# Three kinds of stores of a hybrid decoder kernel are issued from ACT's queue instead of SP's

## The chip, the cores and the metric

The kernel runs on one core of one Trainium2 chip. The time is the device time of one execution in microseconds; a kernel is judged by the median of its runs. Before the change three runs took 1882.16, 1882.66 and 1893.46 us, so the median is 1882.66 us. One execution was profiled.

The core has five engines that run their own instruction streams: PE (matmuls, with PEld for its weight loads), ACT (activations, copies and casts, one input element after the other on 128 partitions), DVE (vector arithmetic), POOL and SP. Each engine has a sequencer, which reads the engine's instructions in order, waits for semaphores and hands the work on. In this kernel SP computes nothing: its sequencer only issues DMA transfers. POOL's issues DMA transfers too, above all the row gathers. ACT's issues none before the change.

## The reference

One layer of a hybrid decoder is applied to 512 prompt tokens and 64 sampled tokens (8 sequences of 8), 576 rows of 1024 floats, all in fp32:

```
proj  = rmsnorm(x) @ w_in                    # q, k, v for 12 heads of 64, and the three conv parts
attn  = merge of three dilated sliding-window attentions (the sample tokens read a cache of 2048 keys)
conv  = B * causal_conv3(C * H)
h     = x + [rmsnorm(attn) | rmsnorm(conv)] @ w_out
xn    = rmsnorm(h)
s     = product keys of xn @ wq              # 8 heads, two halves of 128 keys each
eid,g = top 16 of the 16 x 16 sums per head, softmax over the 16
out   = h + sum over the 128 (head, expert) pairs of g * gelu(xn . u[eid]) * v[eid]
y     = rmsnorm(out)
```

There are 16384 experts, each with one row of u and one of v, of 1024 floats. The outputs are y for both token sets, the new k and v rows, and the conv states.

## The kernel before, in words

The 576 rows are five blocks (`BLKS`): four prompt blocks of 128 rows and the sample block of 64. Precision comes from splitting each fp32 operand into a rounded high part and a rest (`split`, L102 to L104: ACT makes the high part, DVE the rest) and from three matmuls for each product.

The layer's tail (the experts, "PEER") is done in two ways. Blocks 0 and 4 gather, for every one of the 128 pairs, the u and v rows by indirect DMAs from POOL, with dot products and sums on DVE (`gather_units`, L469 to L487). Blocks 1 to 3 (`DENSE`, 384 tokens) use all experts: a matrix G of the gate values, mostly zero, is multiplied into gelu(U x), and the result into V.

The dense way has 128 chunks of 128 experts:

- `ustep(i)` (L773) loads a 512 KB chunk of u to tile `ur` (two buffers, L767, SP), splits it to `uh` and `ul` (two buffers each), does 24 matmuls into `pu` (L107 to L109), and takes the gelu on ACT to tile `a` (L782, 128 x 384). For chunks 0 to 67 (`LAG`) the result must wait until G is ready. Chunks 62 to 67 keep it in SBUF, and chunks 0 to 61 store it to DRAM as `Ad[i]`, 192 KB each, from one of three buffers (L786). These are the stores of U results.
- `gbuild` (L812) makes G for one dense block at a time. For 8 tokens at a time DVE makes one-hot matrices (L844, L848), ACT multiplies the rest of the gate values into them (`oi`, L852, eight activations of 128 x 128), PE multiplies them (`pG`, L857 and L858), and ACT moves the results to `stg` (L860, two activations of 128 x 512). After 32 tokens `stg` (two buffers of 2 MB) is stored as `Gd[...]` (L863). There are 12 of these stores of gates. The loop at L866 calls `ustep` between the pieces of `gbuild`.
- From L933 on, the V stage: U steps 68 to 127 and V steps alternate. Each V step loads a chunk of v, reads back its part of `Gd` (L891) and, for the first 62 chunks, `Ad` (L896), multiplies them on DVE, splits, and does 18 matmuls (L909 to L913).

Ahead of this, `group` (L576) does the output projection, residual and second norm, for block 0 alone and then for blocks 1 to 4. Its inner function `second` (L616) stores the residual rows of a block as `hd` (L619, up to 512 KB, five stores), and goes on with the norm, whose first instruction is a square on ACT (`norm_block`, L157). `hd` is read only at the end (`finish`, L923).

The order of the instructions in each engine's queue is not the order of the text. A planner puts them in order when the program is built, from modelled times: an instruction takes its place when its inputs are modelled as ready, and among ready ones the earlier in the text goes first. On the chip each queue is then strictly in order. A DMA instruction stands in the queue of the engine that issues it, and its wait for the tile that it stores stands there with it. The waits themselves are put in by the builder. Each DMA signals one of eight semaphores for SP's and ACT's transfers together, used in turn, so the issue of one also waits until the earlier user of its semaphore has landed.

Of the kernel before, what the change touches and what calls it, by code (L numbers as in the profile page):

```python
# [19 lines left out]
P = 128  # L20
# [19 lines left out]
TB = 32  # L40
# [27 lines left out]
def body(tc, I, O):  # L68
    nc = tc.nc
# [14 lines left out]
    hd = dram.tile([NTOK, D], F32, name="hd")  # L84
    Ad = dram.tile([LAG, P, ND], F32, name="Ad")
    Gd = dram.tile([NTB, P, NCH, TB], F32, name="Gd")
# [19 lines left out]
    def mm3(out, ah, al, bh, bl, first, last):  # L106
        nc.tensor.matmul(out, ah, bh, start=first, stop=False)  # L107
        nc.tensor.matmul(out, ah, bl, start=False, stop=False)  # L108
        nc.tensor.matmul(out, al, bh, start=False, stop=last)  # L109
# [44 lines left out]
    def norm_block(src, n, gb, out):  # L154
        ss = small.tile([P, 1], F32, name="ss")
        jk = small.tile([P, D], mybir.dt.bfloat16, name="jk", bufs=1)
        nc.scalar.activation(jk[:n], src, AF.Square, accum_out=ss[:n])  # L157
        r = small.tile([P, 1], F32, name="rr")
        rsqrt(r[:n], ss[:n], 1.0 / D, n, 1)
        nc.vector.scalar_tensor_tensor(out, src, r[:n], gb[:n], op0=OP.mult, op1=OP.mult)  # L160

    def transpose_split(xn, n, hi, lo, ps):
        for hf in range(2):
            pt = ps.tile([P, 4, P], F32, name="pT")
            for k in range(4):
                c = hf * 4 + k
                nc.tensor.transpose(pt[:, k, :n], xn[:n, c * P:(c + 1) * P], ident[:n, :n])
            split(hi[:, hf * 4:hf * 4 + 4, :], lo[:, hf * 4:hf * 4 + 4, :], pt[:, :, :n])
# [279 lines left out]
    def pump(cost):  # L448
        credit[0] += cost
        while bg and credit[0] > 0:  # L450
            try:
                c = next(bg[0])
                credit[0] -= c
                left[0] -= c
            except StopIteration:
                bg.pop(0)
        if not bg:
            credit[0] = 0.0
# [117 lines left out]
    def group(grp, st, chp, clp, mm, psc, x2dst, lname, pre2=None):  # L576
# [10 lines left out]
        h = gp.tile([P, nb, D], F32, name="h")  # L587
        for bi, b in enumerate(grp):
            t0, n = BLKS[b]
# [7 lines left out]
        for part, (c0, c1) in enumerate(((0, 6), (6, 8))):  # L597
# [4 lines left out]
            for bi, b in enumerate(grp):  # L602
                t0, n = BLKS[b]
# [12 lines left out]
        def second(bi):  # L616
            b = grp[bi]
            t0, n = BLKS[b]
            nc.sync.dma_start(hd[t0:t0 + n, :], h[:n, bi, :])  # L619
            x2 = x2dst.get(b) if b in x2dst else gp.tile([P, D], F32, name="x2t", bufs=2)  # L620
            norm_block(h[:n, bi, :], n, g2b, x2[:n])
            sl = slice(t0 - g0, t0 - g0 + n)
            transpose_split(x2, n, chp[:, :, sl], clp[:, :, sl], psU)
            pump(PUMP_GB * 2)

        for co in range(2):
            for part, dps in ((1, (3,)), (0, (0, 1, 2))):
# [12 lines left out]
                for bi, b in enumerate(grp):  # L640
                    t0, n = BLKS[b]
# [11 lines left out]
        if one:  # L653
            second(0)
# [8 lines left out]
        if len(grp) == 1:  # L663
            b = grp[0]
            t0, n = BLKS[b]
# [24 lines left out]
        for cc in range(16):  # L690
# [10 lines left out]
            for bi, b in enumerate(grp):  # L701
                t0, n = BLKS[b]
# [5 lines left out]
            for bi, b in enumerate(grp):  # L708
                n = BLKS[b][1]
# [55 lines left out]
    def load_split(src, pl, tag):  # L765
        raw = pl.tile([P, D], F32, name=tag + "r", bufs=RB[tag])
        nc.sync.dma_start(raw, src)  # L767
        hi = pl.tile([P, D], F32R, name=tag + "h")
        lo = pl.tile([P, D], F32R, name=tag + "l")
        split(hi, lo, raw)  # L770
        return hi, lo

    def ustep(i):  # L773
        uh, ul = load_split(I["ut"][i], up, "u")
        uh = uh.rearrange("p (c e) -> p c e", e=P)
        ul = ul.rearrange("p (c e) -> p c e", e=P)
        ps = pu[0].tile([P, 512], F32, name="pu", bufs=2)
        for dc in range(DC):
            mm3(ps[:, :ND], uh[:, dc, :], ul[:, dc, :], x2h[:, dc, :ND], x2l[:, dc, :ND], dc == 0, dc == DC - 1)
        kept = LAG - KEEP <= i < LAG  # L780
        a = up.tile([P, ND], F32, name=f"a{i}" if kept else "a", bufs=1 if kept else AB)
        nc.scalar.activation(a, ps[:, :ND], AF.Gelu)  # L782
        if kept:
            akeep[i] = a
        elif i < LAG:
            nc.sync.dma_start(Ad[i], a)  # L786
        return a

    def unext():
        if ui[0] < LAG:  # L790
            ustep(ui[0])
            ui[0] += 1
            pump(PUMP_WIN)
# [18 lines left out]
    def gbuild(di, b):  # L812
        ef = tk.tile([P, SLOTS], F32, name="ef", bufs=2)
        gt = tk.tile([P, SLOTS], F32, name="gt", bufs=2)
        yield from topk2(st, b, P, ef, gt)
        ei = tk.tile([P, SLOTS], I32, name="ei")
        ii = tk.tile([P, SLOTS], I32, name="ii")
        ij = tk.tile([P, 2, SLOTS], F32, name="ij")
        nc.vector.tensor_copy(ei, ef)
        nc.vector.tensor_scalar(ii, ei, 7, None, op0=OP.logical_shift_right)  # L820
        nc.vector.tensor_copy(ij[:, 0, :], ii)
        nc.vector.tensor_scalar(ii, ei, 127, None, op0=OP.bitwise_and)
        nc.vector.tensor_copy(ij[:, 1, :], ii)
        pt = psG.tile([P, 4, P], F32, name="pT")
        nc.tensor.transpose(pt[:, 0, :], ij[:, 0, :], ident)
        nc.tensor.transpose(pt[:, 1, :], ij[:, 1, :], ident)
        nc.tensor.transpose(pt[:, 2, :], gt, ident)
        JT = gbp.tile([P, P], F16, name="JT")
        J4 = gbp.tile([P, 2, P, 4], F16, name="J4")
        gs = gbp.tile([P, P], F32, name="gs", bufs=1)  # L830
        gl = gbp.tile([P, P], F32, name="gl")
        nc.vector.tensor_copy(JT, pt[:, 1, :])
        nc.vector.tensor_copy(J4[:, 0], pt[:, 0, :].unsqueeze(2).to_broadcast([P, P, 4]))
        nc.vector.tensor_scalar(gs, pt[:, 2, :], GSC, None, op0=OP.mult)
        nc.vector.tensor_copy(J4[:, 1], gs.unsqueeze(2).to_broadcast([P, P, 4]))
        nc.vector.tensor_tensor(gl, gs, J4[:, 1, :, 0], op=OP.subtract)
        yield 1.5
        for tb in range(P // TB):
            stg = gbp.tile([P, NCH, TB], F32, name="stg")
            for q in range(TB // TQ):  # L840
                c0 = tb * TB + q * TQ
                cs = slice(c0, c0 + TQ)
                oj = gbp.tile([P, P, TQ], F16, name="oj")
                nc.vector.tensor_tensor(oj, iotaj, JT[:, cs].unsqueeze(1).to_broadcast([P, P, TQ]), op=OP.is_equal)  # L844
                OI = [gbp.tile([P, 32, TQ, 4], F16, name=f"oi{k}") for k in range(3)]
                f = "p a t b -> p a (t b)"
                for k, in0, op in ((0, iotax, OP.is_equal), (1, OI[0], OP.mult)):
                    nc.vector.tensor_tensor(OI[k].rearrange(f), in0.rearrange(f),  # L848
                                            J4[:, k, cs, :].rearrange("p t b -> p (t b)").unsqueeze(1)
                                            .to_broadcast([P, 32, TQ * 4]), op=op)  # L850
                for tt in range(TQ):
                    nc.scalar.activation(OI[2][:, :, tt, :], OI[0][:, :, tt, :], AF.Copy, scale=gl[:, c0 + tt:c0 + tt + 1])  # L852
                for q4 in range(TQ // 4):
                    pg_ = psG.tile([P, 4, P], F32, name="pG")
                    for t in range(4):
                        tt = q4 * 4 + t
                        nc.tensor.matmul(pg_[:, t, :], oj[:, :, tt], OI[1][:, :, tt, :], start=True, stop=False)  # L857
                        nc.tensor.matmul(pg_[:, t, :], oj[:, :, tt], OI[2][:, :, tt, :], start=False, stop=True)  # L858
                    tl = q * TQ + q4 * 4
                    nc.scalar.activation(stg[:, :, tl:tl + 4].rearrange("p i t -> p t i"), pg_, AF.Copy,  # L860
                                         scale=1.0 / GSC)
                yield 2.5
            nc.sync.dma_start(Gd[di * (P // TB) + tb], stg)  # L863

    debt = 0.0
    for di, b in enumerate(DENSE):  # L866
        for c in gbuild(di, b):
            debt += c
            while debt > WSTEP:
                unext()  # L870
                debt -= WSTEP
# [63 lines left out]
    for n_, i in enumerate(order):  # L935
        if i >= LAG:
            a = ustep(i)
        else:
            a = akeep.get(i)
        v = vprep(i, a)  # L940
        if n_ < NCH - 2:
            for b in range(len(DENSE)):
                vmm(b, v, n_ == 0, False)
        else:
            pend.append(v)
        pump(tail * (RATIO if i >= LAG else 1.0))
# [88 lines left out]
```

## Time and profile before

| | |
|---|---|
| median of 3 runs | 1882.66 us (1882.16 to 1893.46) |
| profiled execution: span | 1882.2 us |
| profiled execution: own time | 1882.16 us by the fastest of the three runs, equal to the span after rounding |
| mean granted TensorE clock | 0.955 of full speed |
| PE busy | 1738.2 us (92%) |
| PE weight loads busy | 1467.3 us (78%) |
| DVE busy | 1430.9 us (76%) |
| ACT busy | 881.6 us (47%) |
| POOL busy | 579.0 us (31%) |
| DMA issued through SP's queue (q1) | 294.22 MB, 44.0% of the 16 DMA engines' time |
| DMA issued through POOL's queue (q0) | 237.69 MB, 35.5% |

How to read it: busy shares are averages over the whole span, and the kernel has stages with different limits. The first U step's gelu starts at 673.7 us, `gbuild`'s activations run from 811.8 to 1079 us, and the first read of `Gd` is issued at 1087.9 us. Matmuls overlap each other, so that a busy PE is not a PE at its peak. A PE clock below 1 is a mean over a stretch in which the chip granted the lower of two levels for part of the time. A DMA instruction's duration is the time that its issue takes the engine's sequencer, not the transfer.

### The profile page before, as it was taken

The numbers are of one execution on the slowest core, as the hardware profiler recorded it, in microseconds if no ns is written. First come the engines' busy times: TensorE is split into PE (matmuls) and PEld (weight loads), VectorE is DVE, ScalarE is ACT, GpSimd is POOL, SyncE is SP. The second block draws the span as 40 slices with busy tenths as digits, with TensorE's granted clock in tenths as the row PEclk, the third lists the DMA queues.
The fourth block names the chain that finished last, engine by engine and source line by source line (L and its number), as shares of the span: only waits on it lengthen the run. The fifth ranks groups of instructions, "written<-read, shape, count | busy, mean of one in ns | idle before, by whom it ended". The sixth has DMA issues, their size and how long they took to land. (4 is left out here: it accounts for less than half of the span.)

```text
span 1882.2 us, 29066 instructions
## 1 busy us (share of the span) xinstructions
PE 1738.2 (92%) x10391; PEld 1467.3 (78%) x10391; DVE 1430.9 (76%) x3064; ACT 881.6 (47%) x1615; POOL 579.0 (31%) x483
## 2 busy tenths in 40 slices
PE   7999899997679999988988999999999999999997
PEld 5778655654558998987978889999999997777776
DVE  5433235766888999998788578888888778888888
ACT  4222366645323333479999933333333333333334
POOL 1010201014554214311212234544444444333330
PEclk9999979978788999999999999999999999999999
DMA  4257569858898448867777699999999999999996
GB/s 143 100 181 288 208 245 337 316 185 291 302 320 302 154 143 312 277 216 267 266 261 250 253 365 330 353 335 348 331 336 341 320 361 334 363 344 367 340 349 210
DMA packets 199077, 533.75 MB, mean 284 GB/s; under 512 B 17586, under 2 KB 82660, under 8 KB 197268
## 3 DMA queue, kind: packets, MB, share of 16 engines
q1 hardware_dynamic: 133364, 294.22, 44.0%
q0 software_dynamic: 65568, 237.69, 35.5%
q8 instruction: 81, 1.33, 0.3%
q14 instruction: 64, 0.52, 0.1%
HBM read 485.65 MB, written 45.63 MB: 282 GB/s over the span
## 5 line engine op out<-in xcount | busy, mean ns | idle before, releaser
L469 POOL DMA_INDIRECT row<-in_u,idxg x192 | 257.9, 1343 | 457.6 <-DVE avg L477 231.4
L469 POOL DMA_INDIRECT row<-in_v,idxg x192 | 264.5, 1377 | 421.6 <-DVE accg L487 345.3
L107 PE MATMUL pu<-x2h,uh 128*128 128x384 f32 x1024 | 350.9, 343 | 21.4 <-ACT a L782 11.1
L109 PE MATMUL pu<-x2h,ul 128*128 128x384 f32 x1024 | 352.0, 344 | 7.5 <-DVE ul L104 7.3
L108 PE MATMUL pu<-x2l,uh 128*128 128x384 f32 x1024 | 348.8, 341 | 0.0
L103 ACT ACTIVATE vh<-vr 128x1024 fp32r<-128x1024 f32 x128 | 135.8, 1061 | 290.4 <-PE y L913 251.4
L477 DVE CUSTOM_DVE_ANT_0 jk<-row,x2g 128x1024 bf16<-128x1024 f32 x192 | 233.8, 1218 | 28.0 <-DMA row<-in_u,idxg 26.8
L487 DVE SCALAR_TENSOR_TENSOR accg<-row,avg,accg 128x1024 f32<-128x1024 f32 x190 | 243.2, 1280 | 7.7 <-DMA row<-in_v,idxg 6.7
L909 PE MATMUL y<-vh,wh 128*128 128x512 f32 x768 | 224.7, 395 | 15.5 <-ACT wh L103 15.5
L911 PE MATMUL y<-vl,wh 128*128 128x512 f32 x768 | 234.2, 393 | 0.0
L107 PEld LDWEIGHTS pu<-x2h,uh 128*128 128x128 f32 x1024 | 196.5, 192 | 27.1 <-ACT a L782 12.2
L104 DVE TENSOR_TENSOR vl<-vr,vh 128x1024 fp32r<-128x1024 f32 x128 | 156.6, 1224 | 77.9 <-ACT vh L103 74.9
L913 PE MATMUL y<-vh,wl 128*128 128x512 f32 x768 | 215.6, 390 | 0.0
L109 PEld LDWEIGHTS pu<-x2h,ul 128*128 128x128 f32 x1024 | 196.4, 192 | 12.4 <-DVE ul L104 10.1
L103 ACT ACTIVATE uh<-ur 128x1024 fp32r<-128x1024 f32 x128 | 136.0, 1064 | 145.1 <-PE pu L108 74.1
L108 PEld LDWEIGHTS pu<-x2l,uh 128*128 128x128 f32 x1024 | 196.3, 192 | 1.7
L104 DVE TENSOR_TENSOR ul<-ur,uh 128x1024 fp32r<-128x1024 f32 x128 | 156.2, 1220 | 35.9 <-ACT uh L103 34.2
L909 PEld LDWEIGHTS y<-vh,wh 128*128 128x128 f32 x768 | 143.9, 189 | 46.5 <-ACT wh L103 19.5
L911 PEld LDWEIGHTS y<-vl,wh 128*128 128x128 f32 x768 | 145.1, 189 | 30.4
L913 PEld LDWEIGHTS y<-vh,wl 128*128 128x128 f32 x768 | 144.0, 188 | 30.1
L104 DVE TENSOR_TENSOR wlo<-wraw,whi 128x1024 fp32r<-128x1024 f32 (+1 forms) x96 | 91.0, 952 | 67.5 <-ACT whi L103 67.1
L103 ACT ACTIVATE whi<-wraw 128x1024 fp32r<-128x1024 f32 (+1 forms) x96 | 79.8, 840 | 124.3 <-PE mm L109 53.7
(281 smaller groups left out, 2936.4 us busy)
## 6 DMA issues: line engine op xcount, KB each, us to landing
ur<-in_ut SPq DMA_DIRECT2D x128, 512.0 KB
vr<-in_v SPq DMA_DIRECT2D x128, 512.0 KB
kt<-in_ck SPq DMA_DIRECT2D x60, 512.0 KB
vt<-in_cv POOLq DMA_DIRECT2D x60, 512.0 KB
Gd<-stg SPq DMA_DIRECT2D x12, 2048.0 KB
gt<-Gd SPq DMA_DIRECT2D x32, 768.0 KB
wraw<-in_w_in SPq DMA_DIRECT2D x24, 512.0 KB
Ad<-a SPq DMA_DIRECT2D x62, 192.0 KB
```

Of the source, the lines that this page charges most:

```text
L103: nc.scalar.activation(hi, src, AF.Copy)
L104: nc.vector.tensor_tensor(lo, src, hi.bitcast(F32), op=OP.subtract)
L107: nc.tensor.matmul(out, ah, bh, start=first, stop=False)
L108: nc.tensor.matmul(out, ah, bl, start=False, stop=False)
L109: nc.tensor.matmul(out, al, bh, start=False, stop=last)
L469: nc.gpsimd.indirect_dma_start(out=r, out_offset=None, in_=I[src], in_offset=bass.IndirectOffsetOnAxis(ap=idx[:, s:s + 1], axis=0))
L477: nc.vector.tensor_tensor_reduce(jk, r, x2, 1.0, 0.0, OP.mult, OP.add, av[:, s:s + 1]))
L487: nc.vector.scalar_tensor_tensor(acc, r, av[:, s:s + 1], acc, op0=OP.mult, op1=OP.add))
L909: nc.tensor.matmul(accs[b][k], wh[:, sl], vh[:, k * 512:k * 512 + 512], start=first, stop=False)
L911: nc.tensor.matmul(accs[b][k], wh[:, sl], vl[:, k * 512:k * 512 + 512], start=False, stop=False)
L913: nc.tensor.matmul(accs[b][k], wl[:, sl], vh[:, k * 512:k * 512 + 512], start=False, stop=last)
```

## The change

Three calls change the engine whose queue issues the DMA, from SP (`nc.sync`) to ACT (`nc.scalar`). Sources, destinations and sizes are the same, and nothing else is edited.

```diff
         def second(bi):
             b = grp[bi]
             t0, n = BLKS[b]
-            nc.sync.dma_start(hd[t0:t0 + n, :], h[:n, bi, :])
+            nc.scalar.dma_start(hd[t0:t0 + n, :], h[:n, bi, :])
...
         if kept:
             akeep[i] = a
         elif i < LAG:
-            nc.sync.dma_start(Ad[i], a)
+            nc.scalar.dma_start(Ad[i], a)
         return a
...
-            nc.sync.dma_start(Gd[di * (P // TB) + tb], stg)
+            nc.scalar.dma_start(Gd[di * (P // TB) + tb], stg)
```

In all 79 DMA instructions move: 62 of `Ad`, 12 of `Gd` and 5 of `hd`.

## Rows read from the trace of the kernel before

**Rows 1.** The page: ACT in the span's 40 slices, busy tenths.
```profile
ACT  4222366645323333479999933333333333333334
```

**Rows 2.** Stretches: time, busy PE, PEld, DVE, ACT, POOL, clock, DMA share, GB/s.
```profile
470.00:564.00 94.00, 66.91 (x304) 50.77 (x304) 81.74 (x160) 32.15 (x57) 52.17 (x39) 0.81 0.87 311
...
660.00:811.00 151.00, 141.30 (x786) 136.54 (x784) 145.91 (x554) 55.56 (x81) 44.62 (x32) 0.98 0.73 240
811.00:1079.00 268.00, 236.60 (x1721) 224.14 (x1722) 220.58 (x461) 259.52 (x567) 56.74 (x33) 0.94 0.72 254
1079.00:1570.00 491.00, 488.83 (x2467) 443.60 (x2465) 398.96 (x453) 174.95 (x237) 223.18 (x168) 1.00 0.95 340
```

**Rows 3.** Waits of PE, 811 to 1079 us: total us, times, longest.
```profile
PE pG L857 <- ACT stg L860: 11.8, 15, 5.1
PE pu L107 <- ACT uh L103: 9.5, 8, 2.2
PE pu L107 <- ACT a L782: 8.6, 4, 2.8
```

**Rows 4.** Waits of ACT, 811 to 1079 us.
```profile
ACT uh L103 <- PE pu L108: 7.8, 2, 5.9
...
ACT uh L103 <- DMA ur<-in_ut: 1.1, 1, 1.1
```

**Rows 5.** Waits of SP's queue, 811 to 1079 us.
```profile
SPq L786 <- ACT a L782: 125.8, 33, 11.1
...
SPq L767 <- DMA ur<-in_ut: 13.9, 6, 5.3
```

**Rows 6.** Line 786 from 811 to 1079 us: durations ns min/median/max, first and last start.
```profile
L786 SPq DMA_DIRECT2D Ad<-a x33: 319/320/327, 811.5 to 1034.9; - x33
L786 SPq EVENT_SEMAPHORE  x15: 17/17/17, 815.6 to 1022.6; - x15
```

**Rows 7.** Lines 863 and 619, the whole span.
```profile
L863 SPq DMA_DIRECT2D Gd<-stg x12: 319/323/327, 837.7 to 1079.0; - x12
...
L619 SPq DMA_DIRECT2D hd<-h x5: 320/327/482, 297.4 to 552.4; - x5
```

**Rows 8.** Line 782 from 910 to 915.5 us: activations and ACT's sequencer (ACTq).
```profile
L782 ACT ACTIVATE a<-pu x2: 467/472/476, 910.4 to 914.9; 128x384 f32<-128x384 f32 x2
L782 ACTq EVENT_SEMAPHORE  x1: 17/17/17, 910.9 to 910.9; - x1
```

**Rows 9.** ACT's instructions from 909.3 us, merged: start, us.
```profile
910.35 0.48 ACT L782 ACTIVATE a<-pu 128x384 f32<-128x384 f32 x1
910.72 2.09 ACT L860 ACTIVATE stg<-pG 128x512 f32<-128x512 f32 x2
912.59 2.41 ACT L852 ACTIVATE oi<-oi,gl 128x128 f16<-128x128 f16 x8
```

**Rows 10.** One gelu and its store, all engines from 900 us.
```profile
902.92 0.47 ACT L782 ACTIVATE a<-pu 128x384 f32<-128x384 f32 x1
...
903.42 0.32 SPq L786 DMA_DIRECT2D Ad<-a  x1
```

**Rows 11.** Line 103 from 906.5 to 910 us: ACT's sequencer and the activation behind it.
```profile
L103 ACTq EVENT_SEMAPHORE  x1: 2067/2067/2067, 907.3 to 907.3; - x1
L103 ACT ACTIVATE uh<-ur x1: 1065/1065/1065, 909.4 to 909.4; 128x1024 fp32r<-128x1024 f32 x1
```

**Rows 12.** Waits of PE, 660 to 811 us.
```profile
PE pu L109 <- DVE ul L104: 5.6, 4, 3.2
PE pu L107 <- ACT a L782: 2.5, 1, 2.5
```

**Rows 13.** Waits of ACT, 660 to 811 us.
```profile
ACT uh L103 <- DMA ur<-in_ut: 30.3, 10, 4.9
```

**Rows 14.** Waits of ACT, 470 to 560 us.
```profile
ACT jk L157 <- DVE h L614: 17.4, 4, 9.6
```

**Rows 15.** Waits of SP's queue, 470 to 560 us.
```profile
SPq L619 <- DVE h L614: 42.8, 4, 30.0
```

## The prediction

> **What bounds the kernel now.** I read the page's 40 slices first. ACT is busy for a third of most slices, but for a block in the middle it stands at 9 [rows 1]. So I cut the span at the events named in the table's text and took the busy times of the stretches, then the waits of each engine in them.
>
> Four stretches matter [rows 2]. From 470 to 564 us the residual rows are made; PE, busy 66.9 of 94 us, waits for the norms. From 660 to 811 us U steps run beside the top-k work: PE is busy 141.3 of 151 us, DVE 145.9, ACT only 55.6. From 811 to 1079 us G is built: ACT is busy 259.5 of 268 us, PE 236.6 at a clock of 0.94. From 1079 to 1570 us PE is busy 488.8 of 491 us; ACT and SP only feed it. The V stage follows and uses none of the moved instructions.
>
> So the stretch from 811 to 1079 us belongs to ACT. The waits agree: PE's three longest there, 11.8, 9.5 and 8.6 us, all end with an ACT instruction [rows 3]. ACT itself is idle for 268 - 259.5 = 8.5 us. The longest wait in its list, 5.9 us, began before 811 us, and only 1.1 us ended with the landing of a u load [rows 4]. SP's queue, on the other hand, stands still a lot: 125.8 us waiting for the gelu whose result it is to store [rows 5]. That looks like the thing to cure, but those waits cost nothing unless a u load behind them comes too late, and that is what 1.1 us says.
>
> **The change, part by part.** It moves 79 issues. Their number by stretch: 33 stores of U results from 811 to 1079 us [rows 6], so 62 - 33 = 29 before that; 12 stores of gates and 5 of residual rows [rows 7]. On SP an issue holds the sequencer for 0.32 to 0.33 us, at most 0.48 among the residual rows [rows 6, 7]. No row shows ACT issuing a DMA; I take SP's duration. Bytes and landing places stay. SP loses the 79 issues and their waits; POOL's queue is not touched.
>
> *U results before 811 us (29).* ACT is idle for 151 - 55.6 = 95 us there [rows 2], which covers 29 x 0.33 = 10 us. If the cover were gone, a split behind a store would start half a microsecond late, and PE would meet it only if it had no prepared u chunk left. What SP's freedom may give back is bounded by PE's waits that a late u load can cause: 5.6 us on `ul`; the 2.5 us on the gelu is ACT's own [rows 12]. ACT waits 30.3 us for u loads in this stretch [rows 13], but nearly all of that dies in the buffers ahead of PE. Between -5.6 and 0 I take -1 us, nearer to nothing, because DVE, busy 145.9 of 151 us, makes `ul` late without SP's help.
>
> *Stores while G is built (33 + 12 = 45).* Here ACT has no idle time to give, so everything hangs on whether an issue costs the engine or only its sequencer. Two rows show the sequencer far ahead of the engine: the semaphore wait that belongs to the gelu of 914.9 us was passed at 910.9 us [rows 8], while two `stg` copies, 2.09 us together, and eight `oi` activations, 2.41 us, stood between the gelu before it and that gelu [rows 9]. A sequencer that is 4 us ahead can spend 0.33 us on a DMA without emptying the engine, if some ACT work lies between the gelu and its store.
>
> Lower bound: a gain of 1.1 us, ACT's whole wait for u loads. Upper bound, with every store right behind the activation that makes its tile: the engine runs dry. From the end of the gelu (902.92 + 0.47) to the issue 0.03 us passed on SP, and the issue took 0.32 [rows 10]. When a wait of the ACT sequencer ended (907.3 + 2.07), the next activation began at 909.4, within 0.05 us [rows 11]. The overlap of neighbours is lost as well: the gelu of 910.35 lasts 0.48 but its follower starts after 0.37, so 0.11 [rows 9]. Together 0.03 + 0.32 + 0.05 + 0.11 = 0.51 us, times 45 = 23 us.
>
> Between -1.1 and +23 I take +2 us. The planner places an instruction when its inputs are modelled as ready, and at the moment when the gelu is issued its store isn't, while the backlog of `stg` and `oi` work is. So the store should come one or more activations later; one `stg` copy, about 1 us, covers an issue. What is left is two semaphore instructions of 17 ns [rows 6] per store: 45 x 2 x 0.017 = 1.5, rounded up.
>
> The Trainium skill speaks against this part (DMA: Bandwidth & Descriptors, section Anatomy of one DMA): a DMA's semaphore wait is made by the issuing sequencer before dispatch, not by the DMA engines. The trace agrees, since the 125.8 us stand in SP's queue [rows 5]. By that alone, with each store next to its gelu, ACT would be held and the sum would be the upper bound's; with work between them the wait is over when the sequencer gets there, and my 2 us stand.
>
> *Residual rows (5).* Four lie from 536 to 552 us. SP waited for the sums on DVE for 42.8 us there, at most 30.0 at once [rows 15]; on ACT the first instruction of the norm waits for the same tile, 17.4 us in four waits [rows 14]. The wait is therefore no new one. The store stands first in the text, so the square starts an issue later: 4 x 0.33 = 1.3 us on the chain for which PE waits; 0 and 5 x 0.48 = 2.4 are the bounds. Loads of `wq` behind SP's wait may come sooner, but their matmuls need all four blocks' norms, so I book no gain.
>
> **Sum.** Span and own time of the profiled execution are 1882.2 us; -1 + 2 + 1.3 gives 1884.5. The median of the runs lies 0.5 us above that execution, so I predict **1885 us**. What is late next is unchanged: ACT until 1079 us, then PE.
>
> The planner adds a spread. Each moved instruction changes modelled times, and neighbours may change places. ACT's idle 8.5 us in its own stretch [rows 2] is what a lucky order could win, and I allow as much for an unlucky one.
>
> **Rivals.**
>
> *Stores right behind their tiles (slower).* Place: ACT's queue from 811 to 1079 us. Mechanism: ACT's sequencer waits for its own engine, which then has nothing to do. Price 0.51 us each, 23 us for 45; 1882.2 - 1 + 23 + 1.3 + 0.5 = 1906 us. It decides when most stores have less than about 0.5 us of ACT work behind the tile's last writer: a lone `oi` of 2.41 / 8 = 0.30 us would not cover one. For it speaks the text's order, store directly after the gelu; against it the backlog and the long run-ahead [rows 8, 9]. Queued behind a held ACT: the `stg` copies for which PE waits and the splits that feed DVE.
>
> *A store waits for an earlier transfer (slower).* The eight DMA semaphores are shared. In SP's queue 13.9 us of waits ended with the landing of an earlier u load, the longest 5.3 us [rows 5]. If the moved issues met as much on ACT, it would be 1882.2 - 1 + 13.9 + 1.3 + 0.5 = 1897 us. Against it: the waits ahead of the 33 stores took 17 ns at most [rows 6], so not one found its semaphore busy.
>
> *SP's freedom pays (faster).* All of PE's 5.6 us on `ul` go [rows 12], and the order turns out well by ACT's 8.5 us: 1882.2 - 5.6 - 8.5 = 1868 us; without the luck 1877. Against it: a u load was the last thing that ACT waited for in only one case of 1.1 us [rows 4]. The Trainium skill holds (DMA: Bandwidth & Descriptors, Issuing engines are not separate DMA queues) that spreading issues over engines saves sequencer time only; by that rule there is nothing to gain but SP's 79 x 0.33 = 26 us, off the path, and 1877 would not be reached.
>
> **How the numbers follow.** Hidden stores, as in the sum: 0.62. Stores right behind their tiles: 0.20. Waits for transfers: 0.08. Faster: 0.10. The range goes from the lucky end of the faster case, 1868, to the exposed stores at 1906. Of this kernel a measurement can tell about 1% from no change, 18.8 us: below 1863.8 or above 1901.5. Faster by more than 1% needs more than any row offers: 0.05. Slower by more than 1%: most of the exposed case and an unlucky part of the second, 0.18. Within 1%: 0.77.
>
> **What would show it.** In the profile after: 79 DMA issues in ACT's queue of 0.32 to 0.48 us each; at least one `stg` copy or split between most gelus and their stores; ACT's busy time and its stretch unchanged within a few microseconds; SP's waits at L786 gone and those at L767 grown in their place, for `ul`. The prediction is wrong if ACT's idle time in the G stage grows by some 0.5 us per store, or if an issue from ACT lasts much longer than one from SP. It is wrong too if more PE idle time there lowers the granted clock, 0.94 now [rows 2], so far that PE becomes the later of the two.

## The result and the profile after

The changed kernel takes **1897.91 us** (median of 8 runs, 1889.59 to 1903.71), the kernel before 1885.07 us (8 runs, 1879.61 to 1893.46). The ratio is 1.0075, 95% interval 1.0053 to 1.0098: slower by a little less than 1%. The profiled execution has a span of 1895.7 us and took 1897.58 us; a run's time is some 1.9 us more than its span, so the execution of before took about 1884 us, not the 1882.16 us of the table above.

First the part to which the prediction gave most of its room. These are the three lines of the stores and the same stretches as in [rows 2], moved by as much as the stage itself has moved (columns as there):

```profile
L786 ACTq DMA_DIRECT2D Ad<-a x62: 321/326/339, 694.4 to 1053.8; - x62
...
L863 ACTq DMA_DIRECT2D Gd<-stg x12: 326/326/327, 844.0 to 1087.9; - x12
...
L619 ACTq DMA_DIRECT2D hd<-h x5: 326/327/507, 301.0 to 567.3; - x5
```

```profile
487.00:581.00 94.00, 64.35 (x296) 49.21 (x296) 75.88 (x150) 30.10 (x53) 44.42 (x34) 0.81 0.87 298
680.00:819.00 139.00, 130.41 (x732) 125.11 (x733) 134.22 (x507) 51.77 (x75) 38.12 (x29) 1.00 0.74 241
819.00:1087.00 268.00, 235.60 (x1709) 222.91 (x1709) 222.70 (x459) 258.28 (x564) 59.84 (x35) 0.94 0.73 258
```

An issue from ACT takes its sequencer as long as one from SP took SP's [rows 6, 7]. The stage in which G is built is unchanged: ACT is busy 258.3 of 268 us (259.5 before), PE 235.6 (236.6), at the same clock. Its length, from the first `oi` to the last `stg`, is 267.4 us against 266.0. PE's waits there answer to [rows 3] one by one, and the wait that SP had at L786 [rows 5] is now one at L767, where SP waits for a free u buffer:

```profile
PE pG L857 <- ACT stg L860: 12.3, 15, 3.4
PE pu L107 <- ACT a L782: 8.6, 4, 2.7
PE pu L107 <- ACT uh L103: 8.1, 4, 2.4
```

```profile
SPq L767 <- DVE ul L104: 207.9, 35, 12.3
...
SPq L767 <- DMA ur<-in_ut: 7.8, 6, 4.2
```

Why ACT loses next to nothing can be seen in its timeline (start, length, engine, line; ACTq is the sequencer). The upper gelu has an `stg` copy between it and its store, as 32 of the 34 stores of U results in this stage have one activation of 1.04 us or more; the lower has none, and ACT stood idle for 0.40 us:

```profile
894.69 0.49 ACT L782 ACTIVATE a<-pu 128x384 f32<-128x384 f32 x1
895.08 1.09 ACT L860 ACTIVATE stg<-pG 128x512 f32<-128x512 f32 x1
895.21 0.33 ACTq L786 DMA_DIRECT2D Ad<-a  x1
895.97 1.18 ACT L860 ACTIVATE stg<-pG 128x512 f32<-128x512 f32 x1
...
899.25 0.46 ACT L782 ACTIVATE a<-pu 128x384 f32<-128x384 f32 x1
899.74 0.33 ACTq L786 DMA_DIRECT2D Ad<-a  x1
900.12 2.00 ACT L860 ACTIVATE stg<-pG 128x512 f32<-128x512 f32 x2 [0.40 <-ACT a L782]
```

**Where the time went.** Starts of the same events in both traces tell it. The first store of residual rows is at 297.4 us before and 301.0 after. The last unit of the sample attention writes its result (`oo`, L277) at 458.3 and 477.2. The first u load is issued at 565.0 and 582.7. From there to the end it is 1317.2 us before and 1313.1 after. So the loss lies ahead of the first u load, and 74 of the 79 moved issues come behind it. Of the 17.7 us that the first u load is late, 3.6 are there at the first store already. Ahead of that store every queue runs in the same order in both kernels, so these 3.6 us are spread between executions and no effect of the change. Counted from the first store, the first u load is issued after 267.6 us before and after 281.7 us in the changed kernel.

It lies in a stretch that the prediction did not read. The planner's order of PE's queue differs from there on (- before, + after; L167 is the transpose of block 0's normed rows, L271 the last product of a sample unit; the list has the program's own matmuls, of which the profile's lines below count two for each one of L271):

```
-L167 MATMUL pT<-ident,x2g_2403 128x128 x8
-L271 MATMUL sT<-vt,PTs 32x128 x24
 L220 MATMUL mm<-ident,sc_2976 128x128 x4
 L228 MATMUL mm<-PT,vtok 64x128
+L271 MATMUL sT<-vt,PTs 32x128 x24
+L228 MATMUL mm<-PT,vtok 64x128 x7
 L249 MATMUL sS<-kt,qbd 32x256 x8
...
+L214 MATMUL mm<-kT,qT 128x256
+L167 MATMUL pT<-ident,x2g_2403 128x128 x8
```

What this does on the chip is seen best around the last two sample units. Before (PE, then POOL, from 430 us): PE's L271 frees three buffers of cached v rows (`vt`), POOL issues the next loads at once, and PE uses them 4 us later. The first row gathers (L469) come after that:

```profile
430.02 1.52 PE L271 MATMUL sT<-vt,PTs 128*32 128x128 f32 x48 [0.38 <-ACT PTs L262]
...
434.90 0.65 PE L271 MATMUL sT<-vt,PTs 128*32 128x128 f32 x16
435.83 0.65 PE L271 MATMUL sT<-vt,PTs 128*32 128x128 f32 x16 [0.29 <-DMA vt<-in_cv]
...
438.99 0.63 PE L259 MATMUL sT<-ident,sc 128*128 128x128 f32 x4
```

```profile
431.00 1.57 POOL L241 DMA_DIRECT2D vt<-in_cv  x3 [7.48 <-PE sT L271]
...
438.03 1.02 POOL L469 DMA_INDIRECT row<-in_u,idxg  x1 [0.70 <-ACT oo L277]
```

After, the same lines: L271 comes 4 to 5 us later, of which 3.6 are the shift that was there at the first store; four gathers stand ahead of the loads in POOL's queue, and 8.4 us pass from the loads' issue to their use. The transposes of the last unit (L259), which stand behind in PE's queue, start at 455.1 instead of 439.0 us:

```profile
433.80 1.06 PE L271 MATMUL sT<-vt,PTs 128*32 128x128 f32 x26
435.81 0.86 PE L271 MATMUL sT<-vt,PTs 128*32 128x128 f32 x22
447.89 1.08 PE L271 MATMUL sT<-vt,PTs 128*32 128x128 f32 x16
449.52 1.08 PE L271 MATMUL sT<-vt,PTs 128*32 128x128 f32 x16
...
455.08 0.66 PE L259 MATMUL sT<-ident,sc 128*128 128x128 f32 x4
```

```profile
434.69 1.02 POOL L469 DMA_INDIRECT row<-in_u,idxg  x1 [11.91 <-DVE mxp L198]
436.02 0.97 POOL L469 DMA_INDIRECT row<-in_u,idxg  x1 [0.30 <-issue]
437.29 0.94 POOL L469 DMA_INDIRECT row<-in_u,idxg  x1 [0.30 <-ACT cat L230]
438.54 0.93 POOL L469 DMA_INDIRECT row<-in_u,idxg  x1 [0.30 <-issue]
439.47 1.15 POOL L241 DMA_DIRECT2D vt<-in_cv  x2
```

PE works on other things meanwhile, at a lower granted clock (third column from the right): 0.83 before and 0.53 after from 440 to 450 us, where 0.5 is the lower of its two levels, 1.2 GHz. In the 15 us ahead of that PE was busy 12.7 us before and 11.3 after:

```profile
425.00:440.00 15.00, 12.68 (x151) 7.87 (x149) 12.14 (x40) 10.97 (x28) 4.30 (x7) 1.00 0.56 203
440.00:450.00 10.00, 8.65 (x78) 5.23 (x79) 6.38 (x14) 4.77 (x12) 5.67 (x7) 0.83 0.83 286
```

```profile
425.00:440.00 15.00, 11.26 (x117) 6.46 (x116) 9.38 (x28) 7.93 (x19) 4.39 (x5) 0.93 0.33 109
440.00:450.00 10.00, 8.25 (x47) 4.25 (x51) 5.58 (x17) 5.13 (x13) 7.16 (x8) 0.53 0.96 363
```

The inputs of blocks 1 to 4 (`h`, L590) wait in SP's queue for the attention's last loads and matmuls. Waits of SP's queue from 430 to 480 us, the first line before, the others after:

```profile
SPq L590 <- DMA vt<-in_cv: 31.5, 1, 31.5
...
SPq L590 <- DMA vt<-in_cv: 56.2, 2, 29.2
SPq L590 <- PE sT L274: 1.4, 1, 1.4
```

The last of the loads of `h` starts at 477.9 us (458.7 before). With that the residual rows, the norms and the first u load are later too. On the page the block of 9s in ACT's row [rows 1] has kept its length:

```profile
ACT  4223366744423333489999933333333333333334
```

### The profile page after: what moved, and what is told of

The parts are those of the page before. It is cut to its first block, busy times and chain, and to the rows that moved or that the text cites. A ratio compares the mean times of both kernels' runs of the same rounds, so it can differ in the third digit from the quotient of the medians.

```text
span 1895.7 us, 28950 instructions
## 1 busy us (share of the span) xinstructions
PE 1740.3 (92%) x10391; PEld 1466.5 (77%) x10391; DVE 1431.4 (76%) x3064; ACT 881.0 (46%) x1615; POOL 577.3 (30%) x483
## 5 line engine op out<-in xcount | busy, mean ns | idle before, releaser
L469 POOL DMA_INDIRECT row<-in_u,idxg x192 | 266.1, 1386 | 483.6 <-DVE avg L477 230.4
L469 POOL DMA_INDIRECT row<-in_v,idxg x192 | 254.5, 1326 | 418.7 <-DVE accg L487 362.1
L103 ACT ACTIVATE wh<-w 128x384 fp32r<-128x384 f32 x128 | 66.3, 521 | 148.0 <-DVE w L898 130.2
```

What stands on the lines that cost most here:

```text
L103: nc.scalar.activation(hi, src, AF.Copy)
L469: nc.gpsimd.indirect_dma_start(out=r, out_offset=None, in_=I[src], in_offset=bass.IndirectOffsetOnAxis(ap=idx[:, s:s + 1], axis=0))
```

## The experiments

Each kernel was timed beside the kernel before on the same chip. The medians of before were 1882.59 us (for five, 74 and one of the stores alone, and for the store behind the norm), 1884.07 (128 x 8, 512 and 1024, and all but block 0's store), 1882.81 (four stores alone, 128 x 256, POOL) and 1886.44 (the last). My theory: what costs is the planner's new order, set off by the stores of residual rows. The rival: what costs is the issue itself in ACT's queue.

**One kind of store alone.** First all five stores of residual rows on ACT, the other 74 on SP.

```diff
-            nc.sync.dma_start(hd[t0:t0 + n, :], h[:n, bi, :])
+            nc.scalar.dma_start(hd[t0:t0 + n, :], h[:n, bi, :])
```

> Only the five stores of residual rows go to ACT. Theory (order): the loss of the change, some 13 us, comes from the residual-row store of block 0, which lets the planner put row gathers ahead of the last vt loads in POOL's queue, so that the sample attention ends some 20 us later; this kernel then has the whole loss, 1895 to 1902 us against 1885. Rival (issue cost): each issue on ACT costs the engine something; five issues of 0.33 us cost at most 2 us, 1885 to 1887.

1891.98 us, 1.0051 (1.0033 to 1.0070). Five issues bring most of the loss; my theory expected all of it, 1895 us or more. Then the opposite, the stores of U results and gates on ACT (74 issues) and the residual rows on SP:

```diff
-            nc.sync.dma_start(Ad[i], a)
+            nc.scalar.dma_start(Ad[i], a)
...
-            nc.sync.dma_start(Gd[di * (P // TB) + tb], stg)
+            nc.scalar.dma_start(Gd[di * (P // TB) + tb], stg)
```

> Only the stores of U results and gates go to ACT (74 issues), the residual rows stay on SP. Theory (order): nothing before 660 us changes and the stores are hidden behind one activation each, so 1880 to 1888 us, no different from before. Rival (issue cost): 74 of the 79 issues are here, so nearly the whole loss, 1895 to 1900 us, most of it from 811 to 1079 us.

1881.30 us, 0.9996 (0.9979 to 1.0013): 74 issues on ACT cost nothing that can be measured. And a single store, that of block 0's residual rows:

```diff
-            nc.sync.dma_start(hd[t0:t0 + n, :], h[:n, bi, :])
+            (nc.scalar if one else nc.sync).dma_start(hd[t0:t0 + n, :], h[:n, bi, :])
```

> A single store goes to ACT, that of block 0's residual rows. Theory (order): the planner's order in POOL's queue is that of the changed kernel, with gathers ahead of the last vt loads, so one moved issue of 0.4 us costs 10 to 18 us: 1894 to 1902. Rival (issue cost): one issue, under 0.5 us: 1885, the same as before.

1892.45 us, 1.0049 (1.0030 to 1.0069), a little under the 1894 us that I expected at least. Moving one issue of 0.35 us costs some 9 us, so the time of the issue itself is out as the cause.

The traces say more than the times here. Up to 544 us every queue has the same order in this kernel, in the one with five stores and in the changed kernel, but for the number of stores moved. Counted from block 0's store, their first u loads are issued after 279.0, 285.3 and 281.7 us. In the three traces with the old order that far (before, 74 on ACT, and 128 x 8 below) it is 267.6, 268.8 and 269.8 us. The new order of this stretch, run three times, is some 13 us later each time than the old one, whether 1, 5 or 79 issues have moved.

**The other four.** Block 0's store stays on SP, the other four go to ACT, first alone and then with the 74:

```diff
+            (nc.sync if one else nc.scalar).dma_start(hd[t0:t0 + n, :], h[:n, bi, :])
```

> The kernel before with four stores on ACT's queue: the residual rows of blocks 1 to 4. Block 0's stays on SP, and so do the stores of U results and of gates. The order differs from that of before only from about 530 us on; POOL's queue is the same. My theory: these four account for the part of the loss that the block 0 store doesn't explain, 1886 to 1892 us, ratio 1.002 to 1.005, lost between 530 and 700 us. Rival (it takes all three kinds together): 1883 to 1885 us, within 0.1% of before.

> 78 of the 79 stores go to ACT as in the change, only block 0's residual rows stay on SP, and POOL's order is the one of before. Theory (order): the loss of the change goes, 1880 to 1888 us, and the sample attention ends at 459 us. Rival (ACT's DMA queue itself costs): 78 of 79 issues cost nearly all of the loss, 1894 to 1900 us.

Alone 1882.53 us, 0.9996 (0.9980 to 1.0012): the theory missed. With the 74: 1888.70 us, 1.0034 (1.0017 to 1.0050), just above the 1880 to 1888 us expected; the attention ended at 466.9 us, not at 459. That profiled execution was the slowest of its twelve (1898.31 us), and it was 7.6 us late at block 0's store already, with the old order up to 530 us. Neither part costs anything measurable alone, and together they do. Effects of re-planning don't add up.

**The order without a DMA on ACT.** All stores stay on SP. One activation is added ahead of block 0's norm, of 128 x 8, 256, 512 or 1024 elements; the norm overwrites its result.

```diff
-            x2 = x2dst.get(b) if b in x2dst else gp.tile([P, D], F32, name="x2t", bufs=2)
+            x2 = x2dst.get(b) if b in x2dst else gp.tile([P, D], F32, name="x2t", bufs=2); one and nc.scalar.activation(x2[:, :512], h[:, bi, :512], AF.Copy)
```

> The same with an activation of 128 x 8 (some 0.2 us); every queue's order is the one of before but for this instruction. Both theories: 1882 to 1885 us, no difference from before. It is the control for the run with 128 x 512.

> The kernel before, all stores on SP, no DMA issued by ACT, with one added activation of 128 x 512 (some 0.6 us of ACT) between block 0's residual-row store and its norm; its output is overwritten. The planner then interleaves row gathers with the last vt loads in POOL's queue, as it does in the changed kernel. Theory (order): the sample attention ends near 478 us instead of 459, and the time is 1890 to 1897 us. Rival (ACT's DMA queue itself costs): there is none here, so only the 0.6 us of work, 1883 us, the same as before.

> The same with an activation of 128 x 1024 (some 1.06 us); the planner's order changes, but in POOL's queue nearly all vt loads stay ahead of the gathers. Theory (order), after the run with the late residual store: the sample attention ends by 466 us, and the time lies anywhere from 1880 to 1898 us, since the order of other instructions changes as well. If POOL's queue alone decides: 1883 to 1887 us. Rival (ACT's DMA queue itself costs): 1884 us, the same as before.

> The kernel before, all stores on SP, with one more activation of 128 x 256 ahead of block 0's norm, whose result is overwritten. The instruction itself takes some 0.3 us. My theory (the order that the planner makes of it decides): 1886 to 1900 us, a ratio of 1.002 to 1.009, as with the activations of 128 x 512 and 128 x 1024. Rival (the losses of those two were chance, and an order of another kind is as often better than the one before): 1873 to 1884 us.

The 128 x 8 kernel, in which the order stays as it was in every queue: 1885.46 us, 1.0000 (0.9980 to 1.0020). 512: 1898.52 us, 1.0086 (1.0068 to 1.0104), for an instruction of 0.62 us. 1024: 1890.03 us, 1.0046 (1.0023 to 1.0070), above the 1883 to 1887 us that POOL's queue alone would give. 256: 1886.41 us, 1.0013 (0.9995 to 1.0031). So a loss of this size needs no DMA on ACT, and the longest activation is not the dearest. Not every new order loses by what can be measured, as the last one shows against my expectation (its time is just inside, its ratio below).

The 128 x 512 kernel does not lose where the changed kernel does. Its attention ends late, at 467.0 us (expected near 478), but its first u load is issued at 557.8 us, earlier than before. Its loss is in the stage in which G is built, 280.0 us from the first `oi` to the last `stg` against 266.0 before. There ACT waits for u loads much longer than the 1.1 us of [rows 4] (the stretch as in [rows 2], then the wait):

```profile
807.00:1089.00 282.00, 250.14 (x1770) 237.36 (x1771) 222.77 (x454) 261.94 (x570) 50.02 (x32) 0.92 0.68 243
```

```profile
ACT uh L103 <- DMA ur<-in_ut: 13.7, 5, 6.8
```

**Another queue.** The five stores of residual rows from POOL:

```diff
+            nc.gpsimd.dma_start(hd[t0:t0 + n, :], h[:n, bi, :])
```

> The kernel before with one change: the five stores of residual rows are issued from POOL's queue, so that no DMA at all is issued from ACT. Only the planner's order differs besides. My theory (a re-planned order costs time, whichever queue the store goes to): 1886 to 1900 us, a ratio of 1.002 to 1.009, with the start of the first u load later than the 565 us of before. Rival (the loss comes from a DMA that stands in ACT's queue ahead of the norm): 1883 to 1885 us, first u load within 3 us of 565.

1881.23 us, 0.9992 (0.9973 to 1.0011). My theory expected a loss; it missed. The order was new here too, but the `vt` loads came ahead of the gathers as before (first gather at 437.5 us, last unit's transposes from 438.3). The rival, that the loss comes from a DMA ahead of the norm in ACT's queue, has it right that nothing is lost, though not the first u load (572.1 us). Against it stands the 128 x 512 kernel: it has no such DMA, and its last sample unit starts 152.9 us behind block 0's store, nearly as late as in the changed kernel (154.1; 141.6 before).

**The stores of residual rows behind the norm.** The changed kernel with the line of all five stores moved below `norm_block`. The square is no longer behind the store, and POOL's queue is nearly that of before.

```diff
-            nc.scalar.dma_start(hd[t0:t0 + n, :], h[:n, bi, :])
             x2 = x2dst.get(b) if b in x2dst else gp.tile([P, D], F32, name="x2t", bufs=2)
             norm_block(h[:n, bi, :], n, g2b, x2[:n])
+            nc.scalar.dma_start(hd[t0:t0 + n, :], h[:n, bi, :])
```

> All 79 stores on ACT as in the changed kernel, but the residual-row store stands behind the norm in the text instead of ahead of it. The number of issues on ACT is the same; the planner's order in POOL's queue is nearly that of before. Theory (order): the loss goes, 1880 to 1890 us. Rival (issue cost): the same 79 issues cost the same, 1895 to 1900 us.

1898.19 us, 1.0073 (1.0050 to 1.0097): a clear miss. The sample attention ended at 462.6 us, as it should, but the first u load came at 575.5 and the way from there to the end took 1324.0 us. No DMA stood ahead of the square of block 0's norm on ACT, and a loss of the same size came about in other places. The rival's time, 1895 to 1900 us, is right, but the 74 issues alone cost nothing and one alone some 9 us, so a cost for each issue is not the reason.

**The late loads.** The changed kernel with the last seven of the 60 `vt` loads issued from SP:

```diff
-            nc.gpsimd.dma_start(vt, I["cv"][pr, bg, kc])
+            (nc.sync if pr == NPAIR - 1 and 2 * kc >= 5 * (1 - bg) else nc.gpsimd).dma_start(vt, I["cv"][pr, bg, kc])
```

> The changed kernel with one more edit: the last seven of the 60 loads of cached v rows are issued from SP's queue instead of POOL's, so that no row gather of POOL can stand ahead of them. ACT's queue is that of the changed kernel up to the attention's last 50 us, with block 0's store in it. POOL theory (in the changed kernel these loads, held up behind gathers, make the sample attention end 22 us late, and that is most of the loss): the sample attention ends at 458 to 468 us instead of 481, the first u load starts at 564 to 573 instead of 583, and the time is 1882 to 1890 us, a ratio of 0.999 to 1.003 to the kernel before. Rival (the loss lies in the order of PE, DVE and ACT, and the late loads only follow from it): the attention ends at 475 or later, and 1893 to 1900 us, a ratio of 1.005 to 1.009.

1897.31 us, 1.0057 (1.0039 to 1.0075), which is the rival's time. The attention ended at 474.1 us, and the place of the loads in POOL's queue falls as the only cause. Up to about 440 us the other queues have the order of the changed kernel, but for the seven loads. In this kernel's timeline (all engines) the loads no longer stand behind a gather. PE uses the first of them earlier than in the changed kernel (443.5 us, not 447.9), but the next no earlier (449.4, not 449.5):

```profile
435.74 1.06 PE L271 MATMUL sT<-vt,PTs 128*32 128x128 f32 x26
436.45 14.47 SPq L241 DMA_DIRECT2D vt<-in_cv  x5
436.62 1.02 POOL L469 DMA_INDIRECT row<-in_u,idxg  x1 [13.03 <-DVE mxp L198]
...
443.51 1.08 PE L271 MATMUL sT<-vt,PTs 128*32 128x128 f32 x16
...
449.44 1.08 PE L271 MATMUL sT<-vt,PTs 128*32 128x128 f32 x16
```

The gathers run at the same time and the loads share the DMA engines with them (busy 1.00 from 440 to 450 us). The Trainium skill says so (DMA: Bandwidth & Descriptors, Issuing engines are not separate DMA queues): whichever engine issues, the transfers interleave on the same 16. This run agrees, with uses at 443.5 and 449.4 us for loads issued from 436.4 on. L271, which frees the buffers, is late here too: counted from block 0's store it starts after 138.4 us (132.6 before). In the changed kernel it started after 132.8 us and its last unit was as late, so a late L271 is not needed for the delay either; most of it passes behind L271.

All kernels at a glance, from one profiled execution each (us):

| kernel | ratio | block 0's store | last unit's transposes start | first u load | from there to the end |
|---|---|---|---|---|---|
| before | | 297.4 | 439.0 | 565.0 | 1317.2 |
| 74 on ACT | 0.9996 | 293.9 | 434.2 | 562.6 | 1312.6 |
| four residual rows on ACT | 0.9996 | 297.1 | 440.5 | 569.8 | 1312.6 |
| residual rows on POOL | 0.9992 | 299.7 | 438.2 | 572.1 | 1311.7 |
| 128 x 8 added | 1.0000 | 294.4 | 436.2 | 564.2 | 1312.4 |
| 128 x 256 added | 1.0013 | 296.8 | 433.1 | 575.3 | 1309.7 |
| all but block 0's store | 1.0034 | 305.0 | 444.5 | 576.3 | 1320.0 |
| 128 x 1024 added | 1.0046 | 295.6 | 426.3 | 570.5 | 1317.5 |
| block 0's store alone | 1.0049 | 297.4 | 453.9 | 576.4 | 1313.4 |
| five residual rows on ACT | 1.0051 | 295.5 | 455.0 | 580.9 | 1309.3 |
| changed, `vt` loads on SP | 1.0057 | 297.3 | 455.1 | 580.9 | 1316.4 |
| changed, stores behind the norm | 1.0073 | 298.4 | 441.0 | 575.5 | 1324.0 |
| changed kernel | 1.0075 | 301.0 | 455.1 | 582.7 | 1313.1 |
| 128 x 512 added | 1.0086 | 296.6 | 449.5 | 557.8 | 1333.8 |

One execution stands in each row, and executions differ. Up to the last unit five kernels have one and the same order (before, 74, four, 128 x 8, all but block 0's store), and their last units start from 434.2 to 444.5 us; counted from block 0's store, from 139.5 to 143.4 us. The five kernels whose last sample unit starts after 449 us (152.9 to 159.5 us behind block 0's store) all lose 0.5 to 0.9%, four of them with the changed kernel's early order; the fifth, 128 x 512, makes the delay up again and loses in the G stage. Of the eight others five lose 0.13% or nothing. The remaining three (1.0034, 1.0046, 1.0073) lose elsewhere. A late first u load does not settle it either: with 128 x 256 it comes 278.5 us behind block 0's store, as late as with that store alone on ACT, and the whole loses 0.13%. No version was measurably faster than the kernel before.

## Why the prediction was right and where it was wrong

The forecast was 1885 us with 1868 to 1906: the time is inside, the likeliest class (within 1%) is the right one, but the value is 13 us too low, and the reason for it was not among the steps. A rise of 2.3 us over the median of before was forecast, and the medians now stand 12.8 us apart. That 1898 lies inside the range is luck: the upper end, 1906, is the price of stores exposed while G is built, and these did not come about.

- **U results before 811 us, -1 us, and stores while G is built, +2 us: right.** Measured together as the 74 issues: 0.9996 (0.9979 to 1.0013), which is -0.8 us with an interval of -4 to +2.4. The two terms add up to +1 us, which lies in the interval; the runs don't tell them apart. The cover was where it was said to be, an activation between gelu and store. The two exceptions, and one of the twelve stores of gates, cost 0.40 us each, near the 0.51 us of the bound.
- **Residual rows, +1.3 us: the step that failed.** Measured alone they cost 1.0051, or 9.6 us (6.2 to 13.2). The prediction priced what the moved instruction does on the chip (an issue ahead of the square) and its price there was right: 0.33 us each. It did not price what the instruction does to the planner, which places block 0's norm a little later at 300 us and then sorts all that follows anew. Three traces with this new order have the first u load some 13 us later than three with the old one.
- **The planner's spread, 8.5 us either way: mis-sized and in the wrong place.** It was taken from ACT's idle time while G is built. The re-sorted stretch that mattered in the changed kernel is the attention, 297 to 480 us, in which the sample unit, the loads and the gathers are tied in a chain; [rows 14, 15] begin only at 470 us. There the new order came 15 us later than the old one to the attention's end, counted from block 0's store (176.2 against 160.9). Nor was the spread even: of the 11 kernels here whose order was clearly new apart from the changed one, none was faster by more than 0.1%, and seven were slower by 0.3 to 0.9%. The order before was a good one among these, but they are not eleven independent tries: three of the losers have the changed kernel's order up to 440 us or further.
- **The rivals.** Stores right behind their tiles: 2 of 34, not most. A store that waits for an earlier transfer: no wait of ACT's sequencer at L786 or L619, one of 17 ns at L863; the time came out near this rival's 1897 us by another cause. SP's freedom pays: SP was free, and waited at L767 instead. The Trainium skill's rule on this (DMA: Bandwidth & Descriptors, same section as above), that spreading issues saves only sequencer time, agrees with the 0.9996.
- **The base.** The run of the profiled execution is about 1.9 us longer than its span, and the median of eight runs is 1885.07 us. The step from span to median, put at 0.5 us, was about 3.

What is shown: the 74 issues on ACT cost nothing measurable; one moved store is enough for most of the loss, and the order of the first 540 us that it sets off is late in each of three traces; an order can cost as much with no DMA on ACT at all, if in another stage. What is read from traces but was not isolated: that the gathers which share the DMA engines with the loads, and in some traces a later L271, are what makes the attention end late. A kernel with the old order and all 79 issues on ACT was not made, so how much of the 1.0075 would be left in it is open; so is where exactly the three other losers lose.

## What to carry to other kernels

A store may be issued from a busy engine's queue for next to nothing, if work that outlasts the issue (0.33 us) stands between the instruction that makes the tile and the store; the covered stores of U results had 1.04 us or more, and how little is enough was not tested. Where a planner orders the queues, price an edit by the stretch that begins where it touches the order first, not only by the stretch where most of the moved instructions lie, and read that stretch's chain too. Here seven of eleven new orders lost and none won, so a new order is a cost to reckon with where the old one has been found good. Compare with a neutral edit (a tiny instruction at the same place) before a difference of under 1% is put down to the edit itself.

## What was not expected of the hardware

- A DMA issue takes ACT's sequencer 0.326 us in the median, as long as SP's 0.320 to 0.327; ACT ran at full load beside 46 of them in one stage (34 at L786, 12 at L863), and the stage took 267.4 us instead of 266.0.
- The same 512 KB loads took 3.9 us from issue to use when no row gather went ahead of them, and 8.4 us behind four; issued from SP's queue while gathers ran, 7.1 us for the first.
- The last sample unit's transposes took 273 ns in the median before, and 421 in the changed kernel and in the one with 128 x 8 added, which is as fast as before. With block 0's store alone on ACT, which is slower, they took 273. So the lower clock in these few microseconds is not what costs the time. In the same columns as the lines of L786, in the window 436 to 470 us, the changed kernel:

```profile
L259 PE MATMUL sT<-ident,sc x11: 272/421/473, 455.1 to 462.4; 128*128 128x128 f32 x10, 128*64 128x128 f32 x1
```

and from 430 to 470 us the kernel with 128 x 8 added:

```profile
L259 PE MATMUL sT<-ident,sc x11: 421/421/476, 436.2 to 444.8; 128*128 128x128 f32 x10, 128*64 128x128 f32 x1
```
